# Seven more pairs of projections by Strassen; v, the conv pairs and all gates ahead of q, k and attention

## The chip, the cores and the metric

The kernel is one layer of an encoder block in float32, in one launch on 1 core of a Trainium2 chip. The metric is the device time of that launch in microseconds. The engines are TensorE (PE, with PEld for its weight loads), VectorE (DVE), ScalarE (ACT), GpSimd (POOL) and SyncE (SP, which only issues transfers here). Every engine runs its own rows in a fixed order and waits for others by semaphores.

## The reference

512 tokens of width 2048; eight heads of 128; a conv branch of 1024 channels and width 31; a feed-forward part of width 5632. Everything is float32.

```python
def rms_norm(x, g):
    xf = x.astype(jnp.float32)
    y = xf * lax.rsqrt(jnp.mean(xf * xf, axis=-1, keepdims=True) + EPS) * g.astype(jnp.float32)
    return y.astype(x.dtype)
...
def neighbourhood_attention(q, k, v, rpb):
...
        s = jnp.einsum('bwhd,biwjhd->bhwij', qr, kw).astype(jnp.float32) * scale
...
        s = s + bias[None].astype(jnp.float32)
        p = jax.nn.softmax(s.reshape(B, H, GRID_W, kr * kc), axis=-1)
...
        return jnp.einsum('bhwij,biwjhd->bwhd', p, vw)
...
def conformer_conv(a, b, w_dw, b_dw, ln_g, ln_b, w_pw):
    z = a * jax.nn.sigmoid(b)
    z = lax.conv_general_dilated(
...
        feature_group_count=z.shape[-1]) + b_dw
    z = layer_norm(z, ln_g, ln_b)
    z = jax.nn.silu(z)
    return z @ w_pw
...
        u = rms_norm(h, mix_pre_g[l])
        proj = u @ w_in[l]
        q, k, v, ca, cb, ga, gb = jnp.split(proj, split_pts, axis=-1)
...
        y_attn = neighbourhood_attention(q, k, v, rpb[l]) @ w_attn_o[l]
        y_conv = conformer_conv(ca, cb, w_dw[l], b_dw[l], conv_ln_g[l],
                                conv_ln_b[l], w_conv_o[l])
        merged = jax.nn.sigmoid(ga) * y_attn + jax.nn.sigmoid(gb) * y_conv
        h = h + rms_norm(merged @ w_out[l], mix_post_g[l])
        u = rms_norm(h, ffn_pre_g[l])
        gate, up = jnp.split(u @ w_gate_up[l], 2, axis=-1)
        f = (jax.nn.silu(gate) * up) @ w_down[l]
        h = h + rms_norm(f, ffn_post_g[l])
```

One input projection gives q, k, v (1024 columns each), the two conv halves (1024 each) and two gates (2048 each).

## The kernel before

**Matmuls in parts.** Activations and weights are split into a high part, rounded to the fast matmul type, and a low part, the difference. A product is then high x high + low x high + high x low: three matmuls of 128 x 512 where one would stand. `wchunk` (lines 138 to 155) loads 1024 columns of weights (512 KB) on SP's queue into a `raw` tile, ScalarE casts them to `whi` (line 148) and VectorE subtracts to `wlo` (line 153). `gemm` (179 to 199) runs one output block of 128 x 512 with 48 matmuls. A "pair" below is two such blocks: the two halves of a conv channel block, or one block of each gate.

**Strassen.** `strassen` makes a pair by Strassen's method in Winograd's form: the pair of weight blocks and the two halves of the contraction and of the tokens are the 2 x 2 blocks, and seven products of 8 matmuls of 512 and 8 of 256 columns (line 293) replace the plain ones. It needs operands made once from the activations (`b11`, `b2`, `t12`, `t34`), four quarters of the weights, sums of them on VectorE (line 277) and one by a transfer that adds onto its destination (line 242, on GpSimd's queue). Results are added and copied at lines 318 to 331 (VectorE), 282 and 300 (ScalarE), and joined at 344.

**The order of the work.** After the start (conv pairs 0 and 1, during which the sums of squares for the first RMSNorm are made on the unnormalised x), conv pairs 2 to 7 run plain; then x is read again and normalised (`normalize`, `un`), with a store to `u_d`; v in two halves, kept in SBUF; then for each head q and k (`qk`, two gemms) and attention. Attention adds a bias plus mask (`bm`, 12 additions a head on GpSimd, line 532, from `braw`, which ScalarE's queue loads), a softmax over VectorE and ScalarE, transpositions (`pt`) on TensorE, and the product with v (`po`). The result goes to DRAM (`att_d`). Then gates 0 and 1 run plain, interleaved in one block of 192 matmuls, while the Strassen operands are made from `u_d`; gates 2 to 15 run as Strassen pairs, their sigmoids going to DRAM (`g_d`). Then the attention outputs come back (`ya`), the conv branch's mean is made (`pmu`, `mu`), and `projected` and `gated` make the 16 blocks `py` of the attention output times the gate (line 766), with the LayerNorm of the conv branch (`cr`, `cv_sq`, `rc`) in steps from block 5 on.

**The taps.** The depthwise convolution of each of the eight conv channel blocks is 30 instructions on VectorE (`taps`, line 447), queued in `todo` and released a few behind each weight chunk: `R_CONV` 4, `R_V` 3 or 4, `R_QK` 4. The last of a block releases an addition to `csum` on GpSimd (line 455) and a store to `c_d`.

**What sets the order.** Each engine's rows are put in order by a scheduler from the program's order and priorities; `keep_in_program_order` and `issued_behind` pin some. Tiles come from pools, so a cast waits until a buffer of its pool is free (`raw` 5, `whi` and `wlo` 3, `bm` 2).

## Time and profile before

| what | value |
|---|---|
| time, median of 2 runs | 2479.15 us (2478.09 to 2480.21) |
| profiled execution, its own time | 2478.69 us |
| its span (first to last instruction) | 2476.9 us |
| mean granted TensorE clock | 0.999 |
| TensorE busy | 2459.8 us (99%) |
| VectorE, ScalarE, GpSimd busy | 2065.7 (83%), 1246.3 (50%), 491.4 (20%) us |
| moved by DMA | 472.84 MB, mean 191 GB/s |

Matmuls are pipelined, so a TensorE that is busy all the time isn't thereby at its peak; what counts here is whether an interval without a matmul stands in its row. In a timeline row stand the start, the length, the engine, the line, the operation and its tiles, and in brackets how long the engine had been idle and what released it. In a row of a group stand the count, the busy time, the mean in ns of one, and the idle time ahead of them.

### The profile page before, as it was taken

How to read it: one execution, taken by the hardware profiler on the slowest of the kernel's cores; microseconds unless marked ns; L12 is line 12 of the kernel's file. 1: busy time of each engine (PE TensorE's matmuls, PEld its weight loads, DVE VectorE, ACT ScalarE, POOL GpSimd, SP SyncE). 2: the span in 40 equal slices, each digit the busy share in tenths (PEclk: the TensorE clock that was granted, in tenths of full speed). 3: DMA queues.
4: the chain of work that ended last, by engine and by line, in shares of the span. 5: the costliest groups of instructions: out<-in, count | busy, mean ns of one | idle time of the engine just before them, and what ended most of it. 6: DMA issues, size and time to landing. Idle time of an engine off the chain costs nothing. (4 is left out here: it accounts for less than half of the span.)

```text
span 2476.9 us, 35440 instructions
## 1 busy us (share of the span) xinstructions
PE 2459.8 (99%) x13171; PEld 2128.0 (86%) x13171; DVE 2065.7 (83%) x2718; ACT 1246.3 (50%) x1924; POOL 491.4 (20%) x575
## 2 busy tenths in 40 slices
...
GB/s 215 90 143 202 105 108 94 132 262 198 191 183 230 190 144 133 201 207 308 156 179 177 184 179 166 182 201 201 207 211 194 214 227 243 244 219 260 211 225 222
DMA packets 162157, 472.84 MB, mean 191 GB/s; under 512 B 18432, under 2 KB 28128, under 8 KB 161984
## 3 DMA queue, kind: packets, MB, share of 16 engines
q1 hardware_dynamic: 106624, 332.57, 39.9%
q0 software_dynamic: 33616, 100.03, 18.9%
...
q14 instruction: 70, 0.57, 0.1%
...
## 5 line engine op out<-in xcount | busy, mean ns | idle before, releaser
L447 DVE SCALAR_TENSOR_TENSOR cv<-z,vec,cv 128x497 f32<-128x497 f32 (+14 forms) x240 | 188.5, 787 | 4.8
L997 POOL TENSOR_TENSOR row<-row,asq 128x512 f32<-128x512 f32 x30 | 55.7, 1855 | 406.4 <-ACT asq L996 406.4
L1158 POOL TENSOR_TENSOR ys<-ys,row 128x512 f32<-128x512 f32 x32 | 57.6, 1800 | 120.0 <-DVE ys L344 101.6
L148 ACT CAST whi_qk<-raw_qk 128x1024 fp32r<-128x1024 f32 x32 | 33.7, 1053 | 79.2 <-PE qk L197 58.1
L153 DVE TENSOR_TENSOR wlo_qk<-raw_qk,whi_qk 128x1024 fp32r<-128x1024 f32 x32 | 40.5, 1264 | 37.8 <-ACT whi_qk L148 37.7
L1021 POOL TENSOR_TENSOR an<-an,row 128x512 f32<-128x512 f32 x32 | 52.3, 1636 | 71.3 <-DMA an<-a_d 44.9
L148 ACT CAST whi_y<-raw_y 128x1024 fp32r<-128x1024 f32 x31 | 32.6, 1051 | 63.1 <-PE py L197 55.2
L532 POOL TENSOR_TENSOR bm<-braw,msk 128x64 f32<-128x64 f32 x96 | 53.5, 591 | 14.8 <-DMA braw<-in_rpb 14.7
L766 DVE TENSOR_TENSOR gg<-py,gg 128x512 f32<-128x512 f32 x32 | 21.8, 687 | 40.3 <-PE py L198 33.2
L197 PE MATMUL py<-ych,whi_y 128*128 128x512 f32 x128 | 49.9, 390 | 0.0
L198 PE MATMUL py<-ych,wlo_y 128*128 128x512 f32 x128 | 49.9, 389 | 0.0
L194 PE MATMUL py<-ycl,whi_y 128*128 128x512 f32 x128 | 49.8, 389 | 0.0
L153 DVE TENSOR_TENSOR wlo_y<-raw_y,whi_y 128x1024 fp32r<-128x1024 f32 x31 | 37.9, 1224 | 14.0 <-ACT whi_y L148 8.6
L455 POOL TENSOR_TENSOR csum<-csum,cv 128x512 f32<-128x512 f32 x7 | 12.7, 1816 | 141.4 <-DVE cv L447 141.4
L148 ACT CAST whi_ca<-raw_ca 128x1024 fp32r<-128x1024 f32 x12 | 12.6, 1053 | 46.3 <-PE cb L197 18.1
L569 ACT ACTIVATE sc<-sc,st 128x256 f32<-128x256 f32 x32 | 16.1, 505 | 30.8 <-DVE st L568 30.8
...
L1159 POOL DMA_DIRECT2D y_d<-ys x32 | 29.4, 918 | 8.1 <-POOL ys L1158 8.1
L148 ACT CAST whi_v<-raw_v 128x1024 fp32r<-128x1024 f32 x16 | 16.8, 1050 | 24.1 <-PE pv L520 17.5
L1088 DVE TENSOR_TENSOR sg<-sg,su 128x512 f32<-128x512 f32 x39 | 28.9, 741 | 0.0
L197 PEld LDWEIGHTS py<-ych,whi_y 128*128 128x128 f32 x128 | 24.0, 188 | 5.0
L194 PEld LDWEIGHTS py<-ycl,whi_y 128*128 128x128 f32 x128 | 24.0, 188 | 5.0
...
## 6 DMA issues: line engine op xcount, KB each, us to landing
raw_qk<-in_w_qk SPq DMA_DIRECT2D x32, 512.0 KB, 3.5
...
raw_v<-in_w_v SPq DMA_DIRECT2D x16, 512.0 KB, 4.4
...
raw_y<-in_w_co SPq DMA_DIRECT2D x16, 512.0 KB, 3.4
raw_f<-in_w_g SPq DMA_DIRECT2D x16, 512.0 KB, 4.3
...
```

What stands on the lines that cost most here:

```text
L148: ins = cast(hi[:, s], raw[:, s])
L153: nc.vector.tensor_tensor(out=lo[:, s], in0=raw[:, s], in1=hi[:, s].bitcast(F32), op=ALU.subtract)
L194: mmul = nc.tensor.matmul(ps, hi[:, s], al, start=first, stop=False)
L197: nc.tensor.matmul(ps, hi[:, s], ah, start=False, stop=False)
L198: nc.tensor.matmul(ps, lo[:, s], ah, start=False, stop=last)
L447: nc.vector.scalar_tensor_tensor(out=a[:, to], in0=z[:, fr], scalar=col(C_WDW, i * CW + w), in1=a[:, to], op0=ALU.mult, op1=ALU.add)
L532: nc.gpsimd.tensor_tensor(out=bm[:, o + i - i0], in0=raw[:, :, min(max(i, 0), 3) * EC : (min(max(i, 0), 3) + 1) * EC], in1=msk[:, o + i - ...
L997: nc.gpsimd.tensor_tensor(out=row[n], in0=row[n], in1=sq, op=ALU.add)
L1021: ins = nc.gpsimd.dma_start(t, a_d[DN_P + k]), nc.gpsimd.tensor_tensor(out=t, in0=t, in1=row[k // KT], op=ALU.mult)
L1088: nc.vector.tensor_tensor(out=t, in0=t, in1=up, op=ALU.mult)
L1158: tc.keep_in_program_order(nc.gpsimd.tensor_tensor(out=t, in0=t, in1=row[n], op=ALU.mult))
L1159: tc.keep_in_program_order(nc.gpsimd.dma_start(y_d[0, o], t, accum_op=ALU.add))
```

## The change

The order of the first third is rewritten. Conv pairs 0 to 2 run plain as before. Then comes v, from the unnormalised u, with the RMSNorm's scale applied when the result is split; v goes to DRAM (`v_d`). During v the operands for Strassen are made (`prepare`, from x read again), and the normalised u is stored to `u_d`. Then 21 Strassen pairs run in a row: conv pairs 3 to 7 and all 16 gates. The products z of the conv pairs go to DRAM (`z_d`) and are fetched when their taps come; three taps are released inside each Strassen pair, behind a matmul of its products 1, 3 and 5.

Then u comes back from `u_d` and is split in place; q and k of heads 0 and 1 are made in one interleaved block of 192 matmuls (`w_q0`); v is loaded back by 16 transfers on GpSimd's queue; and attention follows, with q and k of heads 2 to 7 by `gemm`. In these two the low part of the weights is made by transfer: ScalarE writes minus the weights (a copy with scale -1) rounded to the matmul type, and a transfer on GpSimd's queue reads the weights from DRAM a second time and adds them onto that. `gemm` then runs the low part's eight matmuls behind the sixteen of the high part. The softmax's last scaling goes from VectorE to ScalarE. Five taps are released behind a chunk here, one in v. Attention outputs 6 and 7 are split straight from PSUM; the other six come back from DRAM during head 7. The first four `py` run as one interleaved block (`w_y0`), then `py4` to `py15` as before, with the LayerNorm's steps still from block 5 on.

```diff
-R_CONV, R_V, R_QK = 4, (3, 4), 4
+R_V, R_QK = 1, 5
+PLAIN = 3
+TAP_K, TAP_AT = 2, (1, 3, 5)
+PREPARE = {(0, 1): 0, (0, 3): 1, (0, 5): 2, (1, 1): 3, (1, 3): 4, (1, 4): 5, (1, 6): 6, (1, 7): 7}
+BEFORE = 6
...
+        if by_transfer:
+            nc.scalar.activation(lo, raw, AF.Copy, scale=-1.0)
+            nc.gpsimd.dma_start(lo, src, accum_op=ALU.add)
+        for s in () if by_transfer else parts:
...
+    def split_in_place(t, name):
+
+        hi, lo = slot(f"{name}h", F32R), t.bitcast(F32R)
+        nc.scalar.copy(hi, t)
+        nc.vector.tensor_tensor(out=lo, in0=t, in1=hi.bitcast(F32), op=ALU.subtract)
...
+                    if not by_transfer:
+                        nc.tensor.matmul(ps, lo[:, s], ah, start=False, stop=last)
+                for k in range(w if by_transfer else 0):
+                    ah = acts[c + k][0][:, cols]
+                    nc.tensor.matmul(ps, lo[:, k * P : (k + 1) * P], ah, start=False, stop=c + k == n - 1)
...
+                    if (n, k) == (0, TAP_K) and number in TAP_AT:
+                        taps(1, mmul)
...
+        if i == 0:
+            begin_block(i, z)
+        else:
+            nc.gpsimd.dma_start(z_d[i], z)
+            waiting.append(i)
...
+    def taps(n, behind=None):
+
+        for _ in range(n):
+            if not todo and ahead:
+                begin_block(*ahead.pop())
+            if todo:
+                tap(*todo.pop(0), behind)
+            if len(todo) < BEFORE:
+                fetch()
...
+    def operand(c, r, name):
+
+        t = stp.tile([P, 4, HN], F32, tag="S", name=f"{name}t{c}")
+        t13 = nc.vector.tensor_tensor(
+            out=t[:, :2], in0=r[:, :, B], in1=r[:, 0].rearrange("p (n t) -> p n t", n=2), op=ALU.subtract
+        )
+        b11.append(merged(r[:, 0, A], f"{name}11_{c}"))
+        b2.append([merged(r[:, 1, cols], f"{name}2{c}_{i}") for i, cols in enumerate((A, B))])
+        nc.vector.tensor_tensor(out=t[:, 2], in0=r[:, 1, B], in1=t[:, 0], op=ALU.subtract)
+        nc.vector.tensor_tensor(out=t[:, 3], in0=r[:, 1, A], in1=t[:, 2], op=ALU.subtract)
+        t12.append([merged(t[:, i], f"{name}12{c}_{i}") for i in (0, 2)])
+        t34.append([merged(t[:, i], f"{name}34{c}_{i}") for i in (1, 3)])
+
+    def prepare(c):
+
+        t = stp.tile([P, 2, NT], F32, tag="S1", name=f"un{c}")
+        for j, k in enumerate((c, c + HT)):
+            nc.sync.dma_start(t[:, j], xT[k // 2, :, k % 2 * NT : (k % 2 + 1) * NT])
+            nc.vector.scalar_tensor_tensor(out=t[:, j], in0=t[:, j], scalar=col(C_PRE, k), in1=r1, op0=ALU.mult, op1=ALU.mult)
+        nc.gpsimd.dma_start(u_d[c : c + HT + 1 : HT].rearrange("k p t -> p k t"), t)
+        operand(c, t, "b")
...
+    rate = R_V
+    for i in range(2, PLAIN):
...
+            if (half, c) in PREPARE:
+                prepare(PREPARE[half, c])
...
+        for t in range(NB):
+            for j, part in enumerate(split(pv[t], f"v{half}_{t}", scale=r[:, t : t + 1])):
+                (nc.gpsimd if j else nc.scalar).dma_start(v_d[half, t, j], part.bitcast(F32))
...
+    op = operands(b11, b2, t12, t34)
+    for n in range(CT - PLAIN + KT):
+        i = n + PLAIN
+        w0, w1 = (CT + i, i)
+        if i >= CT:
+            i -= CT
+            w0, w1 = 2 * CT + i, 2 * CT + KT + i
+        gate = n >= CT - PLAIN
+        if n:
+            s1, quarters = sums(w_cg[w1], f"g{n}", load_in_order) if n == 1 else None, None
+        c11, c12, c21, c22 = strassen(
+            w_cg[w0], w_cg[w1], op, f"g{n}", n, s1, quarters=quarters, first=None if n else first, apart=n == 0,
+        )
+        ga, gb = slot(f"ga{n}"), slot(f"gb{n}")
+        joined(ga[:, A], c11)
+        joined(ga[:, B], c12)
+        nc.scalar.activation(ga, ga, AF.Sigmoid)
+        if gate:
+            nc.scalar.dma_start(g_d[i], ga)
+        joined(gb[:, B], c22)
+        joined(gb[:, A], c21)
+        if gate:
+            nc.scalar.activation(gb, gb, AF.Sigmoid)
+            nc.scalar.dma_start(g_d[KT + i], gb)
+        else:
+            glu(i, gb, ga)
...
-            nc.vector.tensor_scalar(out=s, in0=s, scalar1=rs, scalar2=None, op0=ALU.mult)
+            nc.scalar.activation(s, s, AF.Copy, scale=rs)
...
+        if h < H - DIRECT:
+            o = slot(f"ao{h}")
+            nc.scalar.copy(o, po)
+            nc.gpsimd.dma_start(att_d[h], o)
+        else:
+            ya.append(split(po, f"ya{h}"))
...
     rate = R_QK
+    u, v, qk, ya = [], [], [], []
+    pq = [abank(f"qk{h}_{i}") for h in range(2) for i in range(2)]
+    for c in range(HT):
+        for k in (2 * c, 2 * c + 1):
+            t = slot(f"u{k}")
+            load_in_order(t, u_d[k])
+            u.append(split_in_place(t, f"u{k}"))
+        hi, lo = wchunk(w_q0[c], f"q0_{c}", load=load_in_order, by_transfer=True)
+        for part in range(2):
+            for k in range(2):
+                ah, al = u[2 * c + k]
+                for n, ps in enumerate(pq):
+                    s = slice((k * 4 + n) * P, (k * 4 + n + 1) * P)
+                    if part:
+                        nc.tensor.matmul(ps, lo[:, s], ah, start=False, stop=2 * c + k == KT - 1, skip_group_check=True)
+                    else:
+                        nc.tensor.matmul(ps, hi[:, s], al, start=c + k == 0, stop=False, skip_group_check=True)
+                        nc.tensor.matmul(ps, hi[:, s], ah, start=False, stop=False, skip_group_check=True)
+    for half in range(2):
+        v.append([])
+        for t in range(NB):
+            parts = [slot(f"v{half}_{t}{j}", F32R) for j in range(2)]
+            for j, part in enumerate(parts):
+                nc.gpsimd.dma_start(part, v_d[half, t, j])
+            v[half].append(parts)
     for h in range(H):
...
+        if h < 2:
+            bm = bias_of(h)
+            qk = [split(pq[2 * h + i], f"qk{h}_{i}") for i in range(2)]
+        else:
+            bm, qk = bias_of(h), []
+            for i in range(2):
+                ps = bank(f"qk{h}_{i}")
+                gemm([(ps, w_qk[i * H + h])], u, f"qk{h}_{i}", by_transfer=True)
+                qk.append(split(ps, f"qk{h}_{i}"))
+        if h == H - 1:
+            for i in range(H - DIRECT):
+                t = slot(f"ya{i}")
+                load_in_order(t, att_d[i])
+                ya.insert(i, split_in_place(t, f"ya{i}"))
...
+    while todo or waiting or ahead:
+        taps(1)
...
+    py = [bank(f"py{n}_0") for n in range(4)]
+    for c in range(H // 2):
+        hi, lo = wchunk(w_y0[c], f"y0_{c}")
+        for k in range(2):
+            ah, al = ya[2 * c + k]
+            for n, ps in enumerate(py):
+                s = slice((k * 4 + n) * P, (k * 4 + n + 1) * P)
+                nc.tensor.matmul(ps, hi[:, s], al, start=c + k == 0, stop=False)
                 nc.tensor.matmul(ps, hi[:, s], ah, start=False, stop=False)
...
+                nc.tensor.matmul(ps, lo[:, s], ah, start=False, stop=2 * c + k == H - 1)
+    pmu = abank("pmu")
+    nc.tensor.matmul(pmu, ones, csum[0], start=True, stop=True)
...
+    yg += [gated(i, 0, ps, slot(f"gg{i}_0")) for i, ps in enumerate(py)]
+    for i in range(4, KT):
         if LN_AT <= i < LN_AT + 3:
```

**ScalarE, end of the last gate pair.** `g15` (before) and `g20` (after) are the last Strassen pair, `c1` to `c3` copies of its results, `ga` and `gb` the gates; `whi` are casts of the next weights. Before:

```order
L148 CAST whi_y0_0_0_0_7213<-raw_y0_first_7159 128x1024
L300 COPY g15c1_7109<-g15_0_6981 128x256
L300 COPY g15c2_7131<-g15_2_6983 128x256
L148 CAST whi_y1_0_0_0_7244<-raw_y1_0_0_0_7243 128x1024
L148 CAST whi_y2_0_0_0_7278<-raw_y2_0_0_0_7277 128x1024
L712 ACTIVATE mu_7199<-pmu_7197 128x512
L300 COPY g15c3_7153<-g15_1_6982 128x256
L716 ACTIVATE ga15_7201<-ga15_7201 128x512
L717 DMA g_d_4121<-ga15_7201 128x512
L720 ACTIVATE gb15_7202<-gb15_7202 128x512
L721 DMA g_d_4121<-gb15_7202 128x512
L148 CAST whi_y3_0_0_0_7312<-raw_y3_0_0_0_7311 128x1024
```

and after:

```order
L618 ACTIVATE ga20_5384<-ga20_5384 128x512
L620 DMA g_d_1466<-ga20_5384 128x512
L323 COPY g20c3_5382<-g20_1_5208 128x256
L624 ACTIVATE gb20_5385<-gb20_5385 128x512
L625 DMA g_d_1466<-gb20_5385 128x512
L167 CAST u0h_5405<-u0_5403 128x512
L167 CAST u1h_5410<-u1_5408 128x512
L152 CAST whi_q0_0_5414<-raw_q0_0_5413 128x1024
L156 ACTIVATE wlo_q0_0_5415<-raw_q0_0_5413 128x1024
L167 CAST u2h_5453<-u2_5451 128x512
```

Before, casts of the next stage's weights stand ahead of the last copy and the sigmoids; after, the casts of u0 and u1 and of the first weights stand behind them.

**VectorE, head 7's scores.** `qk7_1l` is the low part of head 7's k, which the scores `s7` need; `cv7` rows are taps; `wlo` rows are low parts of weights. Before:

```order
L587 TENSOR_TENSOR ptl6_2_3869<-pt6_2_3864,pth6_2_3868 128x256
L153 TENSOR_TENSOR wlo_g0_0_4134<-raw_g0_0_4127,whi_g0_0_4133 128x1024
L162 TENSOR_TENSOR qk7_0l_3955<-qk7_0_3893,qk7_0h_3954 128x512
L153 TENSOR_TENSOR wlo_g0_1_4192<-raw_g0_1_4161,whi_g0_1_4191 128x1024
L162 TENSOR_TENSOR qk7_1l_4020<-qk7_1_3958,qk7_1h_4019 128x512
L565 SCALAR_TENSOR_TENSOR sc7_0_4027<-s7_0_4023,bm7_3880 128x256
L565 SCALAR_TENSOR_TENSOR sc7_1_4038<-s7_1_4034,bm7_3880 128x256
```

and after:

```order
L490 SCALAR_TENSOR_TENSOR cv7_7179<-zr7_7139,vec_75,cv7_7179 128x504
L490 SCALAR_TENSOR_TENSOR cv7_7179<-zr7_7139,vec_75,cv7_7179 128x503
L160 TENSOR_TENSOR wlo_y0_2_7747<-raw_y0_2_7745,whi_y0_2_7746 128x1024
L490 SCALAR_TENSOR_TENSOR cv7_7179<-zr7_7139,vec_75,cv7_7179 128x502
L176 TENSOR_TENSOR qk7_1l_7549<-qk7_1_7475,qk7_1h_7548 128x512
L490 SCALAR_TENSOR_TENSOR cv7_7179<-zr7_7139,vec_75,cv7_7179 128x501
L490 SCALAR_TENSOR_TENSOR cv7_7179<-zr7_7139,vec_75,cv7_7179 128x500
L490 SCALAR_TENSOR_TENSOR cv7_7179<-zr7_7139,vec_75,cv7_7179 128x499
L490 SCALAR_TENSOR_TENSOR cv7_7179<-zr7_7139,vec_75,cv7_7179 128x498
L168 TENSOR_TENSOR ya0_7552<-ya0_7552,ya0h_7554 128x512
L490 SCALAR_TENSOR_TENSOR cv7_7179<-zr7_7139,vec_75,cv7_7179 128x497
L168 TENSOR_TENSOR ya1_7557<-ya1_7557,ya1h_7559 128x512
```

Low parts of weights stand ahead of it in both. After, a tap does too, and four taps stand between it and the low part of `ya0`, the first operand of `py`. On TensorE 13 matmuls of the plain gates stood between the end of qk7 and `s7` before; after, `s7` follows at once.

**VectorE, start of py.** `gg` rows multiply a finished `py` by its gate, `cr` and `cv0_sq` rows belong to the LayerNorm. Before:

```order
L344 TENSOR_TENSOR gb15_7202<-g15v3_7084 128x256
L344 TENSOR_TENSOR gb15_7202<-g15_1_6982,g15c3_7153 128x256
L766 TENSOR_TENSOR gg0_0_7211<-py0_0_7212,gg0_0_7211 128x512
L153 TENSOR_TENSOR wlo_y3_0_0_0_7313<-raw_y3_0_0_0_7311,whi_y3_0_0_0_7312 128x1024
L731 TENSOR_TENSOR cr0_7377<-cr0_7377,mu_7199 128x512
L731 TENSOR_TENSOR cr1_7378<-cr1_7378,mu_7199 128x512
L731 TENSOR_TENSOR cr2_7379<-cr2_7379,mu_7199 128x512
L731 TENSOR_TENSOR cr3_7380<-cr3_7380,mu_7199 128x512
L731 TENSOR_TENSOR cr4_7381<-cr4_7381,mu_7199 128x512
L731 TENSOR_TENSOR cr5_7382<-cr5_7382,mu_7199 128x512
L766 TENSOR_TENSOR gg1_0_7241<-py1_0_7242,gg1_0_7241 128x512
L153 TENSOR_TENSOR wlo_y4_0_0_0_7347<-raw_y4_0_0_0_7345,whi_y4_0_0_0_7346 128x1024
```

and after:

```order
L812 TENSOR_TENSOR gg0_0_7809<-py0_0_7681,gg0_0_7809 128x512
L812 TENSOR_TENSOR gg1_0_7812<-py1_0_7682,gg1_0_7812 128x512
L812 TENSOR_TENSOR gg2_0_7815<-py2_0_7683,gg2_0_7815 128x512
L812 TENSOR_TENSOR gg3_0_7818<-py3_0_7684,gg3_0_7818 128x512
L777 TENSOR_TENSOR cr0_7853<-cr0_7853,mu_7807 128x512
L160 TENSOR_TENSOR wlo_y4_0_0_0_7825<-raw_y4_0_0_0_7823,whi_y4_0_0_0_7824 128x1024
L777 TENSOR_TENSOR cr1_7854<-cr1_7854,mu_7807 128x512
L777 TENSOR_TENSOR cr2_7855<-cr2_7855,mu_7807 128x512
L777 TENSOR_TENSOR cr3_7856<-cr3_7856,mu_7807 128x512
L777 TENSOR_TENSOR cr4_7857<-cr4_7857,mu_7807 128x512
L777 TENSOR_TENSOR cr5_7858<-cr5_7858,mu_7807 128x512
L422 TENSOR_TENSOR cv0_sq_7870<-cv0_sq_7870,cv1_sq_7873 128x512
```

Before, the low part of the next weights stands behind one `gg`; after, that of `py4` stands behind four `gg` and a `cr`, and more `cr` and sums follow ahead of that of `py5`.

## The prediction

> **What bounds the kernel now.** I read the page first, then TensorE's busy time stage by stage, then what TensorE waited for.

> ```profile
> PE 2459.8 (99%) x13171; PEld 2128.0 (86%) x13171; DVE 2065.7 (83%) x2718; ACT 1246.3 (50%) x1924; POOL 491.4 (20%) x575
> ```

> The view by stages (stretch in us, its length, then busy time of PE, PEld, DVE, ACT, POOL with instruction counts, granted clock, DMA share, GB/s):

> ```profile
> 96.00:183.00 87.00, 87.00 (x386) 72.09 (x385) 85.37 (x105) 21.54 (x25) 14.68 (x10) 1.00 0.39 130
> 270.60:475.80 205.20, 204.94 (x1007) 169.24 (x1006) 149.85 (x275) 69.85 (x140) 65.89 (x141) 1.00 0.29 101
> 489.00:533.00 44.00, 44.00 (x207) 36.91 (x206) 41.12 (x78) 27.38 (x57) 18.76 (x34) 1.00 0.83 276
> 700.00:798.00 98.00, 98.00 (x566) 86.55 (x565) 78.01 (x89) 58.14 (x84) 4.37 (x5) 1.00 0.67 203
> 1605.00:1897.00 292.00, 292.00 (x1676) 257.67 (x1676) 263.92 (x271) 161.17 (x224) 75.42 (x77) 1.00 0.67 202
> ```

> They are: four plain conv pairs; q, k and attention; the plain gates; five Strassen gate pairs; fifteen Strassen pairs of the feed-forward part. In each TensorE is busy for practically the whole stretch at full clock. What TensorE waited for (total, times, longest), longest first; the three rows behind the dots lie in the stretch that the change rewrites:

> ```profile
> PE wo L293 <- DVE m L176: 1.7, 1, 1.7
> ...
> PE pv L520 <- DVE un15l L162: 0.4, 1, 0.4
> PE g L293 <- ACT g2v L282: 0.4, 1, 0.4
> PE g L293 <- DVE g L325: 0.3, 1, 0.3
> ```

> So TensorE's matrix work is the time: fewer columns are a gain, and each new hole in TensorE's row is a loss of its full length. The question is whether the new order makes holes.

> **The saving.** Five conv pairs and gates 0 and 1, seven pairs, go from plain to Strassen. The first row gives 87.00/4 = 21.75 us for a plain pair. A Strassen pair is seven products of 16 matmuls, 112; the last row has 1676/112 = 14.96 pairs in 292.0 us, 19.51 us each (the gate row: 566/112 = 5.05 pairs in 98.0, 19.4). Saving: 7 x 2.24 = 15.7 us. The three waits above go with their stages: 1.1 us. Everything from py15 on is in the same order as before and is costed at nothing, as is the start up to conv pair 1.

> **Vector work inside the pairs.** A pair now carries three taps (line 447 by its instructions: ns minimum, median, maximum), and a conv pair one product z more.

> ```profile
> L447 DVE SCALAR_TENSOR_TENSOR cv<-z,vec,cv x240: 716/743/1784, 63.7 to 406.0; 128x497 f32<-128x497 f32 x8, 128x499 f32<-128x499 f32 x8, 128x501 f32<-128x501 f32 x8, 128x503 f32<-128x503 f32 x8
> ```
> ```profile
> L766 DVE TENSOR_TENSOR gg<-py,gg 128x512 f32<-128x512 f32 x32 | 21.8, 687 | 40.3 <-PE py L198 33.2
> ```

> The gate row has 78.01/5.05 = 15.4 us of DVE a pair; three taps at 0.74 and 0.69 for z make 18.3 of 19.5. The feed-forward row ran with 263.92/14.96 = 17.6 a pair and no stall, so I take 0, and keep 0 to 3 in all. In the v stage 8 x (two normalisations, one subtraction of 1024, two of 256, seven splits of 256) replace 56 taps by 16 and sixteen splits by none; by these durations about as much as leaves. The first Strassen pair follows v with nothing between: its third product waits for an addition and a copy of a result just finished, which I put at 1.3 us (0 to 3), as before's own two waits there were 0.4 and 0.3.

> **First hand-over: last gate pair to q, k of heads 0 and 1.** In the ScalarE rows shown with the change, the casts of u0, u1 and the first weights stand behind the last pair's copy, its sigmoid and its store, and TensorE's next matmul needs them. Before, at the corresponding place (the end of the gates), the next weights had been cast ahead. Timeline of ScalarE and VectorE there (start, length):

> ```profile
> 800.38 0.37 ACT L300 COPY g15c<-g 128x256 f32<-128x256 f32 x1 [0.32 <-DVE ga L344]
> 801.35 0.33 ACTq L717 DMA_DIRECT2D g_d<-ga  x1
> 801.72 0.63 ACT L720 ACTIVATE gb<-gb 128x512 f32<-128x512 f32 x1 [0.40 <-ACT ga L716]
> 804.72 1.05 ACT L148 CAST whi_y<-raw_y 128x1024 fp32r<-128x1024 f32 x1 [2.36 <-PE py L197]
> ```
> ```profile
> 800.87 0.42 DVE L344 TENSOR_TENSOR gb<-g,g15c 128x256 f32<-128x256 f32 x1
> 806.95 3.69 DVE L731 TENSOR_TENSOR cr<-cr,mu 128x512 f32<-128x512 f32 x6
> ```
> ```profile
> L162 ACT CAST qk_1h<-qk 128x512 fp32r<-128x512 f32 x8 | 4.6, 577 | 0.0
> ```

> Copy 0.37, join 0.42, sigmoid 0.63, store issue 0.33, two casts 2 x 0.58, weights 1.05: 3.95, and some 0.25 of hand-offs: 4.2 us. Then the low part: ScalarE writes minus the weights (1.05, as the cast; no row has this operation, a copy of the same size), and a transfer adds the weights onto it. Such accumulating transfers exist in before, at the Strassen sums (queue, size, us from issue to landing):

> ```profile
> g7s<-in_w_cg POOLq DMA_DIRECT2D x1, 512.0 KB, 4.8
> g10s<-in_w_cg POOLq DMA_DIRECT2D x1, 512.0 KB, 7.4
> ```

> 1.05 + 4.8 to 7.4 against 16 matmuls of the high parts that run meanwhile (21.75/96 = 0.227 each, 3.6): 2.2 to 4.8, I take 3.3. [...] By the rows the hand-over costs 7.5 us (6.4 to 9). The seven later chunks of this stage have a chunk of lead and are covered.

> **GpSimd's queue.** On GpSimd's queue, in the new order, sixteen loads of v, one csum and head 0's twelve additions stand ahead of the low part of head 2's first weights. Before had no low part on this queue.

> ```profile
> L455 POOL TENSOR_TENSOR csum<-csum,cv 128x512 f32<-128x512 f32 x7 | 12.7, 1816 | 141.4 <-DVE cv L447 141.4
> 310.43 8.75 POOL L532 TENSOR_TENSOR bm<-braw,msk 128x64 f32<-128x64 f32 x12
> 414.56 3.86 POOL L532 TENSOR_TENSOR bm<-braw,msk 128x64 f32<-128x64 f32 x12 [2.15 <-DMA braw<-in_rpb]
> q1 hardware_dynamic: 106624, 332.57, 39.9%
> q0 software_dynamic: 33616, 100.03, 18.9%
> ```

> While busy, the queues move 332.57 MB/(0.399 x 2476.9 us) = 337 GB/s and 100.03/(0.189 x 2476.9) = 214 GB/s. From the hand-over to the point where TensorE wants that low part (54 us of matmuls and 7.5 of wait) GpSimd's queue moves 8.4 MB (39 us) and SP's about 8 (24 us): 63 for 61.5, so 2 us late (0 to 8; the two can overlap, and both can be slower).

> **Heads 1 to 7.** A head's additions can start only when its bias has landed, issued behind the previous head's output copy (0.58 + 0.33 + 2.5).

> ```profile
> DMA to landing us min/median/max: 2.0/2.5/3.4
> L569 ACT ACTIVATE sc<-sc,st 128x256 f32<-128x256 f32 x32 | 16.1, 505 | 30.8 <-DVE st L568 30.8
> ```

> Heads 1 and 2 have only some 4 us of matmuls between that output and their own scores (before: a head's two gemms, 21.75 us). From there through exponential and the scaling, which is now a ScalarE copy, to the transposition I count 1.6 and 1.2 us late, together 2.8 (0 to 5.5). Heads 3 to 7 have 9 to 13 us, enough for the additions; and 18 to 24 us of matmuls lie between the output and the first low part that stands behind those additions on GpSimd's queue: 0.58 + 0.33 + 2.5 + 3.9 to 8.75 + 4.8 to 7.4 = 12.1 to 19.6, so 0. VectorE loses the low parts and gets one tap more a chunk, and ScalarE, 69.85 of 205.20 busy before, has room for 24 sign copies and 32 scalings.

> **Second hand-over: head 7 to py.** Before, 13 matmuls of the plain gates stood between qk7 and head 7's scores; now none do. The low part of qk7_1 stands on VectorE behind a low part of w_y0 (1.23, its buffer freed only by qk7_1's own end) and a tap: 1.23 + 0.74 + 0.69 = 2.65 us. Then ya0's low part stands behind four taps, 4 x 0.74 + 0.69 against 1.5 of scores (twelve matmuls of 256 at 19.51/7/8 - 0.227 = 0.12): 2.15. Behind the block of py0 to py3 VectorE has four gg, a cr and then the low part of w_y4, then seven more cr and four sums ahead of that of w_y5. In before this same work (the cr row) was spread under py1 to py6.

> ```profile
> 805.80 1.23 DVE L153 TENSOR_TENSOR wlo_y<-raw_y,whi_y 128x1024 fp32r<-128x1024 f32 x1 [0.17 <-ACT whi_y L148]
> ```

> Back to back each takes 3.69/6 = 0.6. The last gg ends 0.75 behind the block, cr 0.6 later, the low part of w_y4 1.2 later: 2.6, less the two matmuls that need only its high part, py4 is 2.15 late. Eleven more at 0.6 and w_y5's 1.2 end at 10.4; py4 ends at 7.6: py5 is 2.4 late. Together 9.3 us (8 to 11).

> **The sum.** -15.7 - 1.1 + 1.3 + 7.5 + 2 + 2.8 + 9.3 = +6.1. The profiled execution took 2478.69 us, span 2476.9; the median is 0.46 above it. So 2478.69 + 6.1 + 0.46 = 2485 us. With the ends, own range: -16.8 + 0 + 6.4 + 0 + 0 + 8 = -2.4, 2477, and -16.8 + 3 + 3 + 9 + 8 + 5.5 + 11 = +22.7, 2502.

> **Rivals.** *The hand-overs are mostly hidden.* If accumulated low parts land in under 4.8 us and the sums of the normalisation don't hold VectorE's row, of the holes only the 4.2 and about 4 at head 7 stay: -16.8 + 8.2 = -8.6, 2470 (2462 to 2477). For it: before lets TensorE wait 1.1 us in 700. Against: the waits are fixed by the order of rows on one engine. *The low parts come late at every head.* They decide once that chain of additions and landing exceeds 18 to 24 us: with additions of 8.75, a csum of 1.8 between and landings of 12 us on crowded queues it is 26, some 5 us late in four heads: 20 us, 2505 (2502 to 2515). For it: additions took 3.86 us without taps beside them and 8.75 with. Against: in the stretch 489 to 533 the DMA moved 276 GB/s and no matmul waited. *Taps hold up the transfers themselves.* If every one of the 32 accumulated low parts of q and k is issued two taps later than I have it (2 x 0.74), and none of that is covered, that is 47 us, 2532; slower than 2% from 1.4 us a chunk on. [...] *The change doesn't do what it says* is excluded by the instructions: 280 matmuls of 512 columns fewer and 392 of 256 more, 7 x (96 - 56) and 7 x 56, as seven pairs give.

> **How the numbers follow.** Forecast 0.57; hand-overs hidden 0.25; late at every head 0.13; taps hold transfers 0.03; anything else 0.02. The range 2464 to 2503 leaves out the lower part of the second case and most of the third and fourth, about 0.2 together; the forecast's own is 2477 to 2502. About 2% (50 us) is what a measurement tells from no change: to be faster by that needs 33 us more than all the columns saved, 0.01; slower by it only the fourth case and some of the rest, 0.04; within, 0.95.

> **What would show it.** Right: 21 Strassen pairs in a row at 19.5 us with TensorE without holes; a hole of about 7.5 us in two pieces at the first q0 matmuls, waiting for ScalarE and then for a transfer; waits for VectorE's qk7_1l, ya0 and the low parts of w_y4 and w_y5. Wrong: pairs of 20 us and more (VectorE is the bound there); waits for low parts inside every head; or none of the holes, with the span near 2462.

## The result, and the profile after

The changed kernel took 2513.9 us (median of 2 runs, 2512.86 to 2514.94) against 2479.15: ratio 1.014, 95% interval 1.0097 to 1.0184. It is slower by 35 us, and the forecast of 2485 us (2464 to 2503) was 29 us too low. The profiled execution's span went from 2476.9 to 2510.8 us, 33.9 more.

The page of the changed kernel, its span and its first line of busy times, and the mean granted clock (0.999 before):

```profile
span 2510.8 us, 36051 instructions
PE 2460.0 (98%) x13283; PEld 2130.0 (85%) x13283; DVE 2078.6 (83%) x2756; ACT 1334.3 (53%) x2063; POOL 511.9 (20%) x614
core 0: 2510.8 us, clock 0.992
```

TensorE is busy no longer than before (2459.8), although seven pairs are cheaper: 15.7 us of its columns are gone, and most of that has come back as slower columns (below). The rest of the loss is idle time. The view by stages of the changed kernel shows where (stretch, its length, busy time of PE, PEld, DVE, ACT, POOL, granted clock, DMA share, GB/s); the stretches are v, the 21 Strassen pairs, q and k of heads 0 and 1, the heads, and the first `py`:

```profile
74.00:161.00 87.00, 87.00 (x386) 72.06 (x385) 73.40 (x130) 39.05 (x78) 8.76 (x13) 1.00 0.65 209
161.20:570.90 409.70, 409.70 (x2353) 361.42 (x2351) 358.60 (x426) 222.57 (x308) 24.39 (x32) 1.00 0.62 185
570.90:640.20 69.30, 56.21 (x227) 44.38 (x226) 41.67 (x61) 34.09 (x43) 25.77 (x47) 0.93 1.01 304
640.20:807.20 167.00, 157.76 (x782) 129.41 (x781) 125.24 (x242) 92.62 (x177) 69.83 (x137) 0.98 0.72 172
807.20:860.00 52.80, 40.43 (x167) 30.84 (x166) 31.55 (x55) 20.27 (x38) 8.10 (x13) 0.87 0.51 167
```

Up to 570.9 us all is as forecast: 409.70/21 = 19.51 us a pair, no hole. Behind it TensorE idles for 13.1, 9.2 and 12.4 us in the three stretches, and for the first time the granted clock is below 1. What TensorE waited for between 500 and 900 us (total, times, longest):

```profile
PE qk L723 <- DMA wlo_q<-in_w_q: 9.0, 5, 5.2
PE pt L692 <- ACT sc L680: 8.5, 4, 3.4
PE py L213 <- DVE wlo_y L160: 4.3, 2, 3.1
PE qk L725 <- ACT whi_q L152: 4.1, 1, 4.1
PE py L208 <- ACT whi_y L152: 3.3, 1, 3.3
PE s L663 <- DVE qk_1l L176: 3.2, 2, 3.0
PE py L762 <- DVE ya L168: 1.6, 1, 1.6
PE qk L208 <- ACT whi_qk L152: 0.5, 1, 0.5
```

These are 34.5 us. Before, the same stretch had 0.7.

**The clock.** The waits are not all of it. Around the longest hole, the stretch before the clock falls, the slow one, and the one behind it:

```profile
624.50:627.50 3.00, 0.50 (x3) 0.07 (x1) 0.00 (x0) 0.50 (x1) 0.94 (x2) 1.00 1.08 286
627.50:634.40 6.90, 4.22 (x10) 3.36 (x11) 0.00 (x0) 0.40 (x1) 3.52 (x9) 0.51 1.19 382
634.40:640.00 5.60, 5.60 (x26) 4.59 (x26) 1.29 (x2) 2.69 (x4) 5.53 (x17) 1.00 1.00 265
```

For 6.83 us the granted clock is one half. The trace's record of the clock has seven such stretches in this kernel behind the start, at 576.3, 627.5, 665.1, 685.6, 811.9, 846.0 and 1218.0 us, each 3.41 or 6.83 us long, 34.1 us together; the kernel before has none ahead of its last 10 us. In them matmuls start 0.43 us apart in place of 0.227 (two of q0's first matmuls, start and length, from the timeline of TensorE):

```profile
576.66 0.63 PE L726 MATMUL qk<-u0h,whi_q 128*128 128x512 f32 x1
577.09 0.63 PE L725 MATMUL qk<-u,whi_q 128*128 128x512 f32 x1
```

8.6 us of the 34.1 are idle anyway (they lie in holes), so the half clock costs (34.1 - 8.6)/2 = 12.8 us. The account of the 33.9: -15.7 (pairs), -1.1 (waits gone), +34.5 (waits), +12.8 (clock), +1.5 (a hole at 1215 us, where TensorE waits for the sums of squares of the feed-forward norm) = 32.0; 1.9 us I can't assign. The forecast had 22.9 us of waits and nothing for the clock; so of the 29 us that it is too low, 11.6 are waits and 12.8 the clock.

**The places, in the order of the program.** The lengths given from here on are counted between the starts of two matmuls, less the time of one; they come out a little longer than the waits of the view above, some 37 us in all for its 34.5. The first hand-over, timeline of ScalarE:

```profile
571.18 0.37 ACT L323 COPY g20c<-g 128x256 f32<-128x256 f32 x1 [1.27 <-PE g L314]
572.04 0.63 ACT L624 ACTIVATE gb<-gb 128x512 f32<-128x512 f32 x1 [0.49 <-DVE gb L367]
...
574.17 1.04 ACT L152 CAST whi_q<-raw_q 128x1024 fp32r<-128x1024 f32 x1
```

TensorE's hole there is 4.17 us; 4.2 had been counted. Then low parts that come by transfer are late five times: 1.45 us for the first chunk of q0, 1.14, 1.32 and 0.52 for the next three, and 5.35 for the last, whose transfer took 15.4 us from issue to landing. The DMA rows of the changed kernel (queue, count, size, median us to landing):

```profile
wlo_qk<-in_w_qk POOLq DMA_DIRECT2D x24, 512.0 KB, 8.1
u<-u_d SPq DMA_DIRECT2D x16, 256.0 KB, 9.9
raw_q<-in_w_q SPq DMA_DIRECT2D x8, 512.0 KB, 11.5
wlo_q<-in_w_q POOLq DMA_DIRECT2D x8, 512.0 KB, 8.9
```

With all 16 engines busy (share 1.01, 304 GB/s) an accumulating transfer of 512 KB takes 8.9 us (median of the eight, 5.6 to 15.4), not the 4.8 to 7.4 that the two rows of before had shown. At heads 1, 2 and 3 transpositions wait for scores whose bias is late, by 3.11, 3.52 and 1.73 + 0.80 us. At head 2 the bias's load is issued at 674.13 and GpSimd starts the additions at 681.03, after 5.17 us of idle time (timeline of ScalarE's queue and of GpSimd):

```profile
674.13 0.36 ACTq L637 DMA_DIRECT2D braw<-in_rpb  x1
```
```profile
681.03 4.71 POOL L641 TENSOR_TENSOR bm<-braw,msk 128x64 f32<-128x64 f32 x12 [5.17 <-DMA braw<-in_rpb]
```

At the end of head 7, k's low part costs 3.17 and `ya0` 1.80 us. `py4` then waits twice, 3.49 us for its high part and 3.50 for its low part. SP's queue tells why the first came late, and ScalarE's row what it waited for:

```profile
833.80 0.33 SPq L259 DMA_DIRECT2D wo0s<-in_w_out  x1
...
836.71 0.43 SPq L819 DMA_DIRECT2D raw_y<-in_w_ao  x1
```
```profile
844.59 1.04 ACT L152 CAST whi_y<-raw_y 128x1024 fp32r<-128x1024 f32 x1 [4.36 <-DMA raw_y<-in_w_ao]
```

Two loads for the output projection, far ahead of their use, go into memory that attention still holds until 833.8 us (SP stands still for 40.2 us ahead of the first); the load of `py4`'s weights stands behind them on SP's queue.

### The profile page after: what moved, and what is told of

The parts are those of the page before. It is cut to its first block, busy times and chain, and to the rows that moved or that the text cites. A ratio compares the mean times of both kernels' runs of the same rounds, so it can differ in the third digit from the quotient of the medians.

```text
span 2510.8 us, 36051 instructions
## 1 busy us (share of the span) xinstructions
PE 2460.0 (98%) x13283; PEld 2130.0 (85%) x13283; DVE 2078.6 (83%) x2756; ACT 1334.3 (53%) x2063; POOL 511.9 (20%) x614
## 5 line engine op out<-in xcount | busy, mean ns | idle before, releaser
L490 DVE SCALAR_TENSOR_TENSOR cv<-zr,vec,cv 128x498 f32<-128x498 f32 (+14 forms) x210 | 157.5, 758 | 2.2
L208 PE MATMUL qk<-u,whi_qk 128*128 128x512 f32 x192 | 76.9, 400 | 0.5 <-ACT whi_qk L152 0.5
L641 POOL TENSOR_TENSOR bm<-braw,msk 128x64 f32<-128x64 f32 x96 | 47.2, 525 | 31.0 <-DMA braw<-in_rpb 31.0
L812 DVE TENSOR_TENSOR gg<-py,gg 128x512 f32<-128x512 f32 x32 | 21.8, 688 | 30.4 <-PE py L213 25.6
L208 PEld LDWEIGHTS qk<-u,whi_qk 128*128 128x128 f32 x192 | 37.0, 193 | 7.7 <-ACT whi_qk L152 0.7
L152 ACT CAST whi_qk<-raw_qk 128x1024 fp32r<-128x1024 f32 x24 | 25.3, 1053 | 29.8 <-PE qk L211 22.7
L156 ACT ACTIVATE wlo_qk<-raw_qk 128x1024 fp32r<-128x1024 f32 x24 | 25.4, 1060 | 14.4 <-DMA v<-v_d 9.0
L208 PE MATMUL py<-ya,whi_y 128*128 128x512 f32 x72 | 29.0, 403 | 3.3 <-ACT whi_y L152 3.3
L157 POOL DMA_DIRECT2D wlo_qk<-in_w_qk x24 | 21.4, 955 | 51.3 <-ACT wlo_qk L156 42.4
L696 DVE TENSOR_TENSOR ptl<-pt,pth 128x256 fp32r<-128x256 f32 x32 | 12.5, 420 | 22.9 <-ACT pth L695 22.8
L725 PE MATMUL qk<-u,whi_q 128*128 128x512 f32 x64 | 26.0, 406 | 4.1 <-ACT whi_q L152 4.1
L152 ACT CAST whi_v<-raw_v 128x1024 fp32r<-128x1024 f32 x16 | 16.8, 1052 | 23.8 <-PE pv L585 14.9
## 6 DMA issues: line engine op xcount, KB each, us to landing
raw_qk<-in_w_qk SPq DMA_DIRECT2D x24, 512.0 KB, 5.4
wlo_qk<-in_w_qk POOLq DMA_DIRECT2D x24, 512.0 KB, 8.1
raw_v<-in_w_v SPq DMA_DIRECT2D x16, 512.0 KB, 3.7
raw_y<-in_w_co SPq DMA_DIRECT2D x16, 512.0 KB, 3.6
raw_f<-in_w_g SPq DMA_DIRECT2D x16, 512.0 KB, 4.3
```

Source lines behind the costliest of these rows:

```text
L152: ins = cast(hi[:, s], raw[:, s])
L208: mmul = nc.tensor.matmul(ps, hi[:, s], al, start=first, stop=False)
L490: ins = nc.vector.scalar_tensor_tensor(out=a[:, to], in0=z[:, fr], scalar=col(C_WDW, i * CW + w), in1=a[:, to], op0=ALU.mult, op1=ALU.add)
L641: nc.gpsimd.tensor_tensor(out=bm[:, o + i - i0], in0=raw[:, :, min(max(i, 0), 3) * EC : (min(max(i, 0), 3) + 1) * EC], in1=msk[:, o + i - ...
```

## The experiments

The theory after seeing the trace: the change saves its 15.7 us, and all of the loss is holes in q0's stage, the heads and the first `py`, plus the half clock behind them. The rivals differ from run to run: that another wait stands behind each hole, that the transfers and not the order are the loss, that the half clock has another cause. In the tables "waits" is the sum of TensorE's waits between 500 and 900 us as above, and "half clock" the time at half the clock, without the start and the end. All edits are against the changed kernel if nothing else is said.

### Holes filled with idle work

Eighteen transpositions into an unused bank are put behind the last gate pair and thirteen behind head 7's last gemm; they compute nothing that is used.

```diff
+    filled(FILL[0], "fill0")
     pq = [abank(f"qk{h}_{i}") for h in range(2) for i in range(2)]
...
         if h == H - 1:
+            filled(FILL[1], "fill1")
```

> The changed kernel with idle work for TensorE in two of its holes: 18 transpositions of a constant behind the last Strassen pair, 13 behind the end of head 7's k; nothing waits for them and no wait is taken away. Theory A (TensorE's clock is halved for some microseconds after a hole of 3 us and more): the matmuls behind both places run at 0.23 us instead of 0.43, and the time falls by about 4 us to 2510. Rival (the slow matmuls have another cause, such as the crowded DMA or the restart of the engine after a wait): they stay at 0.43 and the time stays within 1 us of the changed kernel, 2514.

Measured: 2511.39 us, ratio 1.0127 (1.0110 to 1.0144). At head 7 the half-clock stretch of 6.83 us is gone and the matmuls behind run 0.23 us apart. At the first place a hole of 2.20 us was left behind the transpositions, and the clock fell for 3.41 us all the same. Half clock in all 23.9 us, waits 34.6. So filling helps where it covers the idle time and not where 2 us stay; with a gain of 2.5 us against runs that scatter from 2506.6 to 2515.7 the time itself decides little.

### The bias one head earlier

```diff
+    ahead_bm = [bias_of(0)]
     for h in range(H):
+        bm = ahead_bm.pop(0)
+        if h + 1 < H:
+            ahead_bm.append(bias_of(h + 1))
```

> The changed kernel with each head's bias loaded and added one head earlier. Theory A (the bias is late, because its load is issued behind the previous head's output): the holes ahead of the transpositions of heads 1, 2 and 3 (3.1, 3.5 and 1.7 + 0.8 us) go, and the half-clock windows behind the first two: 10 to 12 us, 2502 to 2504. Rival (the softmax's own chain on VectorE and ScalarE sets them): the holes stay, the change is under 3 us, 2511 to 2514.

Measured: 2509.9 us, ratio 1.0122 (1.0107 to 1.0137). The waits for scores at heads 1 to 3 fall from 8.5 to 0.5 us, so the late bias was their cause. The time fell by only 4 us of the 10 to 12 of the theory: the half clock grew from 34.1 to 37.6 us, and a new wait of 3.4 us stands at head 4, for k's low part, behind a tap that waits for its reloaded z (timeline of VectorE in this run):

```profile
724.19 0.55 DVE L479 TENSOR_SCALAR cv<-zr,vec 128x512 f32<-128x512 f32 x1 [3.20 <-DMA zr<-z_d]
...
728.24 0.68 DVE L176 TENSOR_TENSOR qk_1l<-qk,qk_1h 128x512 fp32r<-128x512 f32 x1
```

### The loads of v behind the last low part of q0

```diff
-                nc.gpsimd.dma_start(part, v_d[half, t, j])
+                issued_behind(nc.gpsimd.dma_start(part, v_d[half, t, j]), added[-1])
```

> The changed kernel with the sixteen loads of v issued behind the last low part of the q0 stage, on the same queue. Theory A (the order in GpSimd's queue makes the hole of 5.4 us ahead of the last low part): the hole falls under 2 us, and with its half-clock window 4 to 7 us are gained, 2507 to 2510. Rival (all 16 DMA engines are busy and the bytes are the same): the wait moves to head 2's low part or to the product with v, and under 2 us are gained, 2512 to 2515.

Measured: 2513.31 us, ratio 1.0135 (1.0118 to 1.0152), no gain. The hole of 5.35 us is gone (1.34 stand near there, for a cast of the next weights), and one of 3.87 us opens at the next transferred low part:

```profile
643.93 0.80 PE L218 MATMUL qk<-u0h,wlo_qk 128*128 128x512 f32 x1 [3.81 <-DMA wlo_qk<-in_w_qk]
```

Head 2's hole grows from 3.52 to 4.94 as well. What one transfer gains another loses, as the rival said: the order on GpSimd's queue alone was not the limit.

### The output projection's sums loaded later

```diff
-        s1 = s1 or sums(w1, name)
+        s1 = s1 or (sums(w1, name, load_late) if name in ("wo0", "wo2") else sums(w1, name))
```

`load_late` issues the load behind the seventeenth of the gates' loads.

> The changed kernel with the two early loads for w_out, which wait for memory that attention holds, issued behind the gate loads of the second half of py instead of ahead of py4's weights on SP's queue. Theory A (that queue is blocked, so py4's weights and the LayerNorm's rows come late): the two holes of 3.5 us at py4 shrink to at most the 2.2 and 2.4 of the prediction, and the half-clock window goes: 4 to 7 us less, 2507 to 2510. Rival (VectorE's order alone sets these holes): under 2 us, 2512 to 2515.

Measured: 2507.15 us, ratio 1.0113 (1.0098 to 1.0128). The 3.49 + 3.50 us at `py4` become one hole of 2.23, for VectorE's low part of w_y4, and `py5`'s 1.40 becomes 0.77. That is the hole that the prediction had counted (2.15); the wait on SP's queue stood in front of it unseen. The half clock behind it is one window shorter, but in the whole kernel it is 34.1 us as before.

### The first hand-over brought ahead

The first q0 chunk's splits and cast are issued ahead of the last pair's copy, joins and sigmoid.

```diff
+            if early and i == 3:
+                issued_behind(ins, casts[-1])
...
+        if early:
+            early()
```

> Edit: the first q0 chunk is begun before the last Strassen pair is joined, so that u0's and u1's high parts and q0's first cast stand on ScalarE ahead of that pair's copies, joins and sigmoid; nothing else moves. Theory (the sum of after's time is holes of TensorE plus half-clock windows behind them): the hole of 4.17 us at 570.9 falls under 1, that of 1.45 at 580.4 too, since the first low part's transfer is issued earlier, and the half-clock window of 6.8 us at 576 goes: 4.2 + 1.4 + 3.4 = 9 off, of which up to 3 may come back where the later low parts are still late: 2505 to 2508. Rival (the later low parts set the stage, since the DMA engines are full from 570 to 640): the first holes go and the later ones grow by as much; 2511 to 2515.

Measured: 2505.47 us, ratio 1.0104 (1.0087 to 1.0121), 8 us off. The hole of 4.17 goes, and so do those of 1.45 to 0.52 and that of 5.35; in their place one of 5.42 stands at the second chunk's low part. Of 4.1 + 9.0 us of waits in this stage 5.3 are left. The theory's time came out, but half of what the rival says too: a transferred low part is still late.

### q0's low parts by VectorE

```diff
-        hi, lo = wchunk(w_q0[c], f"q0_{c}", load=load_in_order, by_transfer=True)
+        hi, lo = wchunk(w_q0[c], f"q0_{c}", load=load_in_order)
...
-R_V, R_QK = 1, 5
+R_V, R_Q0, R_QK = 1, 3, 6
```

> Edit: q0's low parts are made by VectorE's subtraction again, not by transfers; for that the taps are given fewer turns in q0's stage (three a chunk instead of five) and six in each head's. Theory (DMA: the low parts are late because all 16 engines carry u, raw weights, v and the accumulating transfers at 301 GB/s): the five holes behind low parts, 1.45 + 1.14 + 1.32 + 0.52 + 5.35 = 9.8 us, fall under 4 in sum, and the half-clock window at 627 goes (1.7 to 3.4 us): 2503 to 2508, if no tap becomes late at the heads. Rival (u's and raw loads themselves are late, whoever makes the low part): the holes stay, named by other waits, above 7 us: 2510 to 2515.

Measured: 2511.18 us, ratio 1.0129 (1.0114 to 1.0144). All holes behind q0's low parts go, but the half clock grows from 34.1 to 37.5 us, and transpositions and scores in the heads are late now by 10.8 + 10.7 us in place of 8.5 + 3.2. The rival's time came out, but not its reason. Whether six taps a chunk are too many there isn't shown: the run "The heads' transfers alone" below has five and loses as much to k's low part. Of the longest waits here, the 4.6 us at 730 us are for a bias, and the 4.3 at 700 for k's low part, behind a late reload of z and nine taps (timeline of VectorE in this run):

```profile
696.86 0.55 DVE L479 TENSOR_SCALAR cv<-zr,vec 128x512 f32<-128x512 f32 x1 [4.02 <-DMA zr<-z_d]
```

### All transfers undone

```diff
-        hi, lo = wchunk(w_q0[c], f"q0_{c}", load=load_in_order, by_transfer=True)
+        hi, lo = wchunk(w_q0[c], f"q0_{c}", load=load_in_order)
...
-                gemm([(ps, w_qk[i * H + h])], u, f"qk{h}_{i}", by_transfer=True)
+                gemm([(ps, w_qk[i * H + h])], u, f"qk{h}_{i}")
```

> Edit: the changed kernel with that part undone that makes low parts by transfers (q0's eight and the heads' twenty-four); order, taps and all else stay. VectorE has 32 x 1.2 = 38 us more between 570 and 800, ScalarE 32 x 1.05 = 34 us less, the DMA queues 16.8 MB less. Theory (late low parts and the half clock behind them cost the changed kernel some 12 us in q0's stage and 1 in the heads, but VectorE at 53.6 of 60 us in the heads can't take 29 us more): q0's holes go, the heads' grow: 2510 to 2530. Rival (the transfers are the loss): 2495 to 2505.

Measured: 2492.05 us, ratio 1.0059 (1.0042 to 1.0075), 22 us faster than the changed kernel: the transfers are most of the loss, the rival was right, and by more than it said. (In `gemm` the matmuls of the low part stand beside those of the high part again; that order wasn't tried by itself.) VectorE takes the 38 us of subtractions without becoming the bound; from 570 to 640 us the view by stages of this run and of the changed kernel read

```profile
570.00:640.00 70.00, 62.47 (x282) 50.88 (x280) 65.43 (x98) 30.07 (x50) 24.11 (x36) 0.98 0.71 243
```
```profile
570.00:640.00 70.00, 56.91 (x233) 45.07 (x232) 41.67 (x61) 34.09 (x43) 25.77 (x47) 0.93 1.00 301
```

with VectorE at 65.43 of 70 us and the DMA engines at 0.71 in place of 1.00. Other transfers land sooner, u in 5.4 us in place of 9.9 and q0's weights in 6.3 in place of 11.5 (DMA rows of this run). Waits 20.5 us, half clock 17.1.

```profile
u<-u_d SPq DMA_DIRECT2D x16, 256.0 KB, 5.4
raw_q<-in_w_q SPq DMA_DIRECT2D x8, 512.0 KB, 6.3
```

### The heads' transfers alone

Only q0's eight low parts go to VectorE; the taps stay as in the changed kernel.

> Edit: the changed kernel with q0's eight low parts made by VectorE; the heads' twenty-four stay transfers. Undoing both gave 2492, none 2514. Theory (q0's stage is where the DMA engines are full, and q0's eight are the loss): 2492 to 2499. Rival (the heads' transfers, which load the queues while biases and v land, are the loss): 2504 to 2512.

Measured: 2515.18 us, ratio 1.0139 (1.0123 to 1.0156). The rival again, and a little above it: taking the transfers from q0 alone gains nothing, and the heads' 24 transfers alone cost 23 us against none. In q0's stage u and the weights now land in 5.2 and 6.2 us and the holes for low parts are gone; the heads, where the DMA share is 0.68 between 640 and 700 us against 0.33 without transfers, now have 7.5 us of waits for the transferred low parts of weights and 11.3 for k's own low part. The longest of these, 5.9 us at 694 us, is for VectorE's taps, which wait for a reload of z that stands on SP's queue behind weight loads which wait for a buffer (timeline of SP's queue and of VectorE in this run):

```profile
661.40 22.87 SPq L151 DMA_DIRECT2D raw_qk<-in_w_qk  x4
684.38 1.38 SPq L473 DMA_DIRECT2D zr<-z_d  x1
```
```profile
693.78 0.55 DVE L479 TENSOR_SCALAR cv<-zr,vec 128x512 f32<-128x512 f32 x1 [5.38 <-DMA zr<-z_d]
```

### By what the transfers cost

Two runs ask whether the transfers cost because matmuls wait for what they make, or because of what they do to others. In the first every transfer is replaced by a plain load of the same 512 KB that nobody reads; in the second all transfers stay, but make a tile that no matmul reads. VectorE makes the low parts in both; `idle` is a tile of its own with four buffers. The edits, shortened:

```diff
         if by_transfer:
-            nc.scalar.activation(lo, raw, AF.Copy, scale=-1.0)
-            nc.gpsimd.dma_start(lo, src, accum_op=ALU.add)
+            nc.gpsimd.dma_start(idle, src)
```
```diff
-            nc.scalar.activation(lo, raw, AF.Copy, scale=-1.0)
-            nc.gpsimd.dma_start(lo, src, accum_op=ALU.add)
+            nc.scalar.activation(idle, raw, AF.Copy, scale=-1.0)
+            nc.gpsimd.dma_start(idle, src, accum_op=ALU.add)
```

> Edit: no low part is made by a transfer (VectorE makes all), but in the place of each of the 32 accumulating transfers GpSimd's queue issues a plain load of the same 512 KB into a tile that nothing reads. Theory (the transfers cost by their bytes: 16.8 MB more between 570 and 800, the DMA engines full from 570 to 640, so u, raw weights, v and the bias land later): 2503 to 2513, the heads' holes behind late biases back at 3 us each. Rival (they cost by the low part's own late landing, for which matmuls wait): 2490 to 2497, as without transfers (2492).

> Edit: all 32 transfers of the changed kernel stay, with ScalarE's negated copy ahead of each and at its place in GpSimd's queue, but they make a tile that no matmul reads; VectorE makes the low parts that are read, as in the kernel without transfers (2492). Theory (the transfers cost by what they do to others: raw weights, u, v, biases and z land later, ScalarE has 34 us more): 2505 to 2515, near the changed kernel's 2514. Rival (they cost by the low part's own late landing): 2490 to 2497.

Measured: 2515.28 us (ratio 1.0139, 1.0124 to 1.0154) and 2526.16 us (1.0190, 1.0169 to 1.0212). Both are far above the 2492 without transfers, although no matmul waits for a transferred low part in either. So transfers cost by what they do to others too, and not only where a matmul waits for what they make. The waits of the second run, the largest three:

```profile
PE pt L693 <- ACT sc L681: 11.9, 4, 4.7
PE s L664 <- DVE qk_1l L177: 10.0, 4, 3.2
PE po L699 <- DVE ptl L697: 7.3, 2, 4.3
```

How the changed kernel's loss splits stays open, since each edit brings a loss of its own. In the first run most of these loads, which wait for no weights, were issued at once, ahead of v's and the bias, on GpSimd's queue; that makes one hole of 12.9 us at the scores of an early head, with 17.1 us of half clock around it, some 16 us together, without which the run would be near 2499 (an estimate), between the theory and the rival. What the bytes did to q0 is plainer: its weights land in 14.9 us, and TensorE waits 9.7 us for their high parts, 4.1 of which are the hand-over's. In the second run ScalarE waited for earlier transfers into the tiles that it was to write next, up to 2.5 us each between 644 and 661 us, so it is dearer than the changed kernel was.

### The order mended

The pieces above together: the hand-over brought ahead, q0's low parts by VectorE, the bias one head earlier, w_out's sums later, z's reloads begun sixteen taps ahead instead of six, three taps a chunk in q0 and six in the heads. A second kernel keeps the transfers in q0, with five taps.

```diff
-R_V, R_QK = 1, 5
+R_V, R_Q0, R_QK = 1, 3, 6
...
-BEFORE = 6
+BEFORE = 16
```

> Edit: the hand-over brought ahead, q0's low parts by VectorE, taps three a chunk in q0 and six a head, each head's bias made one head earlier, the sums of w_out's quarters loaded later, z's reloads started sixteen taps ahead instead of six. Theory (nothing but these waits and the half clock behind them lies between after and the pairs' saving): the holes fall from 38.5 us to under 12 and the half-clock windows from 30.7 us to under 7; 2479.2 - 15.7 + 1.6 + 12 + 2 = 2479, with 2470 to 2485 as bounds. Rival (the stage of q0 and the heads is short of DMA or of VectorE whatever the order): the holes move to other places and stay above 25 us; 2492 to 2505.

> The same kernel as the last, but with q0's low parts still made by transfers and five taps a chunk. Theory: the low parts' holes stay (4 to 9 us, and one half-clock window more): 5 to 10 us above the last kernel, 2478 to 2492. Rival (VectorE is the scarcer of the two): no slower than the last kernel or faster than it.

Measured: 2486.65 us (ratio 1.0030, 1.0019 to 1.0042) and 2497.0 (1.0073, 1.0058 to 1.0088). Waits 16.6 and 25.7 us, half clock 10.2 and 23.9. So 27 us of the loss go, somewhat less than the theory had (2470 to 2485). Transfers in q0, with five taps a chunk in place of three, cost 10 us here, where they cost nothing beside the heads' transfers in the unmended order (2513.9 against 2515.2). That other holes hid them there is a guess. Of the 16.6 us, 6.7 are GpSimd's memsets of the scores, queued behind a bias that hasn't landed:

```profile
PE pt L719 <- POOL sc L698: 6.7, 2, 3.8
```

The next pair loads each bias two heads ahead and moves taps from the heads to q0 (six a chunk there, five in the heads); the second of the two has no transfer left at all.

```diff
+        if h + 2 < H:
+            raw_of(h + 2)
+        bm = ahead_bm.pop(0)
```

> Edit: as the mended kernel, with each bias's load issued two heads ahead and its sum one head ahead, and six taps a chunk in q0's stage and five a head's chunk (three and six there). Theory (the mended kernel's remaining 19.2 us of holes are GpSimd's wait for a bias's load, with the memsets of the scores behind it, and VectorE's taps ahead of scores and k's low part): the holes of 3.96, 3.03, 1.49 us go and those of 3.07 and 1.88 shrink to 3 together; 8 to 10 us of holes stay, hardly a half-clock window: 2472 to 2478, the first below the kernel before. Rival (VectorE in q0's stage is then the late one): q0's low parts wait for taps; holes move to 570 to 635, sum above 16: 2482 to 2490.

> The same kernel, but the heads' low parts of q and k weights are made by VectorE too, so no low part by a transfer is left. VectorE then has 24 subtractions of 1.2 us = 29 us more in about 165 us of heads, where it was busy 53.2 of 60 us. Theory (the transfers pay here): VectorE becomes the bound of the heads, holes grow by 8 to 20 us: 2482 to 2496. Rival (the transfers give nothing, their gain is eaten by late landings): within 4 us of the kernel beside it.

Measured: 2488.72 us (1.0038, 1.0023 to 1.0053) and 2482.19 us (1.0012, 1.0003 to 1.0022). The waits for the bias are gone, and the rival of the first came true: in both, TensorE waits at the end of q0 for a low part of u, as VectorE has nine taps ahead of it (timeline of VectorE, the kernel without transfers):

```profile
610.49 5.95 DVE L502 SCALAR_TENSOR_TENSOR cv<-zr,vec,cv 128x505 f32<-128x505 f32 x9
616.35 0.69 DVE L170 TENSOR_TENSOR u<-u,u14h 128x512 fp32r<-128x512 f32 x1
```

Without transfers the kernel is 6.5 us faster, not slower: against both theories all 24 of the heads' transfers lose even here.

The last pair adds a fourth tap to each Strassen pair, three or four taps a chunk in q0, and the LayerNorm's steps one block later; the first keeps transfers in heads 4 to 7 alone, the second has none.

```diff
-LN_AT = 5
+LN_AT = 6
...
-TAP_K, TAP_AT = 2, (1, 3, 5)
+TAP_K, TAP_AT = 2, (1, 3, 5, 6)
...
-                gemm([(ps, w_qk[i * H + h])], u, f"qk{h}_{i}", by_transfer=True)
+                gemm([(ps, w_qk[i * H + h])], u, f"qk{h}_{i}", by_transfer=h >= 4)
```

> Edit: as the second mended kernel, but a fourth tap in each Strassen pair (21 taps fewer for the heads), three taps a chunk in q0 and six a head's chunk, the layer norm of the conv output one block later, and transfers only in heads 4 to 7, where the DMA engines have room (share 0.36 in the heads without transfers). Theory (the holes left are VectorE's taps ahead of u14's, k7's and py4's low parts): holes 18.4 or 16.4 us fall to 8 or less and at most one half-clock window stays: 2468 to 2476, faster than the kernel before. Rival (a fourth tap makes the pairs late, or six a chunk the heads): 2479 to 2488.

> The same with no transfer at all, four taps a chunk in q0 and five a head's chunk. Theory (VectorE, busy 56.7 of 60 us in heads 3 to 5 without transfers, keeps up since 21 taps have gone to the pairs): within 3 us of the kernel beside it, 2468 to 2478. Rival (VectorE is the bound of the heads): 4 to 10 us slower than it.

Measured: 2471.47 us, ratio 0.9961 (0.9946 to 0.9976), and 2472.38 us, 0.9965 (0.9953 to 0.9977). Both are faster than the kernel before, by 10 and 9 us against its 2481.46 beside them (0.4%), as the theories had it; and transfers in heads 4 to 7 alone neither gain nor lose. Stages and all waits of the first (q0, heads, first `py`):

```profile
572.40:621.10 48.70, 48.70 (x217) 40.18 (x217) 45.05 (x58) 20.08 (x28) 29.95 (x46) 1.00 0.87 295
621.10:779.00 157.90, 157.58 (x792) 128.86 (x792) 126.50 (x244) 88.09 (x173) 57.86 (x130) 1.00 0.68 174
779.00:830.00 51.00, 47.50 (x218) 38.29 (x218) 32.02 (x55) 21.90 (x40) 0.39 (x1) 0.97 0.46 165
```
```profile
PE s L696 <- DVE qk_1l L178: 2.2, 2, 2.0
PE py L215 <- DVE wlo_y L162: 1.5, 1, 1.5
```

From the end of the pairs to the first scores the changed kernel took 69.3 us, for 227 matmuls; this one takes 48.7, for 217, and one half-clock window is left.

| kernel | time, us | waits 500 to 900, us | half clock, us |
|---|---|---|---|
| before | 2479.2 | 0.7 | 0 |
| changed | 2513.9 | 34.5 | 34.1 |
| no transfers | 2492.1 | 20.5 | 17.1 |
| mended | 2486.7 | 16.6 | 10.2 |
| mended, transfers in q0 | 2497.0 | 25.7 | 23.9 |
| mended 2 | 2488.7 | 14.5 | 13.7 |
| mended 2, no transfers | 2482.2 | 12.9 | 3.4 |
| mended 3 | 2471.5 | 3.7 | 3.4 |
| mended 3, no transfers | 2472.4 | 7.6 | 6.8 |

2479.2 - 15.7, plus the waits, plus a little under half of the half-clock time gives each row below the first within 5 us, the changed kernel's 2513.9 as 2498.0 + 12.8 = 2510.8.

### The clock by itself

Here the edit is to the kernel before. Eleven holes are put into the dense feed-forward pairs: between the halves of one product ScalarE copies the tile that both read onto itself, and the next matmul waits for it.

```diff
+                for _ in range(copies if n == 0 else 0):
+                    nc.scalar.copy(op[b][0], op[b][0].bitcast(F32))
```

> Edit: the kernel before, with eleven holes put into TensorE's dense stream, one in each of the pairs f6 to f16 (19.5 us or more apart): between the halves of one product, ScalarE copies the tile that both read onto itself two to seven times over, which the next matmul has to wait for; the order of the matmuls is otherwise unchanged, and nothing else is left out. Holes of about 1.5 to 4.5 us, 30 us in sum. Theory (a hole costs more than its length, because the clock is granted for windows of 3.41 us on a fixed grid by what TensorE did in the window before): no half-clock window behind holes under 2 us, one behind some of 2.5 to 4 us by where they fall on the grid, one behind each longer than 4 us; starts of half-clock windows lie at whole multiples of 3.413 us from each other; each window of 3.41 us costs 1.7 us: 30 us + 5 windows x 1.7 = 2515 to 2525. Rival (a hole costs its length; the half-clock windows come from something else, such as the transfers' load): 2505 to 2512, no half-clock window.

Measured: 2540.26 us, ratio 1.0247 (1.0227 to 1.0268). The holes came out longer than meant, 2.33 to 5.58 us, 42.2 together, and the span rose by 62.0 (2476.9 to 2538.9): nearly half as much again as the holes. The trace has ten half-clock stretches, behind ten of the eleven holes, 51.2 us together, fifteen windows where the theory had five for its shorter holes; 7.7 of them lie in holes, so (51.2 - 7.7)/2 = 21.8, and 42.2 + 21.8 = 64 for 62.0 measured. The rival, that a hole costs its length, would have given 2521. Two holes of this run in the view by stages: each row is 3.41 us of the grid on which the half-clock stretches start.

```profile
1276.97:1280.38 3.41, 1.99 (x10) 1.30 (x8) 2.97 (x3) 1.85 (x4) 1.04 (x2) 1.00 0.40 127
1280.38:1283.80 3.42, 2.33 (x18) 2.29 (x19) 1.01 (x1) 1.63 (x3) 0.00 (x0) 1.00 0.91 160
...
1300.86:1304.28 3.42, 0.60 (x3) 0.22 (x2) 0.76 (x1) 2.70 (x4) 0.75 (x1) 1.00 0.60 95
1304.28:1307.69 3.41, 3.41 (x17) 3.41 (x17) 1.61 (x2) 0.59 (x1) 0.00 (x0) 0.50 0.68 213
```

The hole of 2.68 us at 1278.8 lies across two windows, 1.59 and 1.09 us, and costs its length. The one of 2.98 us at 1301.1 lies in one, and the next window runs at half clock. A hole of 2.33 us, 2.28 of it in one window, was followed by half clock, too.

## Why the prediction was wrong

**Right: what is saved.** "Seven pairs, 7 x 2.24 = 15.7": 21 pairs at 19.51 us, no hole, and the last mended kernels, 9 to 10 us faster than the kernel before, show that most of the saving is there to be had. The term for v to the first pair (1.3) was 0.

**Right in place, and mostly in size: the waits that were read off the order of one engine.** The hand-over's ScalarE chain, 4.2 against 4.17; k's low part at head 7, 2.65 against 3.17; `ya0`, 2.15 against 1.80; `py4`'s low part, 2.15 against 3.50, and 2.23 once the wait in front of it was taken away; `py5`, 2.4 against 1.40, 1 us too much. The first low part by transfer, 3.3 against 1.45, was put too high.

**Wrong: "every hole is a loss of its full length".** That sentence, under what bounds the kernel, is the first step that failed: the half clock behind the holes cost another 12.8 us, and no term and no rival held it. The waits that the prediction found in the profile before were 1.7 us at most, and no half clock follows them; the edited kernel before shows that a dense kernel without any of the new order pays for longer holes in the same way.

**Wrong: "the seven later chunks of this stage have a chunk of lead and are covered".** Three of them cost 3.0 us together, and the last 5.35, since transfers land in 9 to 12 us here with all engines busy (the medians above are 8.9, 9.9 and 11.5), and that one in 15.4. The queue term (2 us, 0 to 8) put the lateness at the low part of head 2's first weights, where no matmul waited, and it had too few bytes: some 16.4 MB for 61.5 us, where 21.05 MB went through between 570 and 640 us. The landing of 4.8 to 7.4 us came from transfers at 590 and 649 us of the kernel before, where the DMA share was 0.63 (570 to 700 us), not 1.

**Wrong in size: heads 1 to 3.** 2.8 us had been counted for heads 1 and 2, with a bias that lands in 2.0 to 3.4 us. At head 2 it took nearly 7, and head 3, counted as safe, lost 2.5 more: 9.2 in all. The run with the bias a head earlier shows that this wait was the cause.

**Not seen: SP's queue at `py4`.** 3.49 us of waiting and the half clock behind it. The prediction treated SP's queue as a rate and not as an order in which one blocked load stops the next.

**VectorE's relief was not what the profile asked for.** The prediction costed a transfer only where a matmul waits for what it makes. Without transfers VectorE is busy 57.2 of 60 us in heads 3 to 5, and TensorE still 59.45. The rival "the low parts come late at every head" (0.13, 2502 to 2515) holds the measured time, but by luck: in the changed kernel no matmul of heads 2 to 7 waits for a transferred low part. 9.0 us of its waits are for those of q0; the rest of what the transfers cost came through other loads (u, weights, biases) or through ScalarE's 34 us of copies (32 of 1.05 us), and how much through each isn't shown. The rival that taps hold up the transfers was not tried by itself, but in q0's stage the trace speaks against it: GpSimd issued all eight transfers within 0.3 us of the end of ScalarE's copy, and not two taps, 1.5 us, behind it.

**The range.** The waits by themselves would have given 2498, inside it, though 11.6 us of waits more than forecast had used up most of the room. The clock took the time out of it.
